# Half-size weight loads in six buffers, and attention bias rows repeated in memory instead of squares made by matmul

## The chip, the core and the metric

The kernel runs on one core of one Trainium2 chip. The metric is the time of one execution on the device in microseconds (us); a lower time is better. Three runs of the kernel before took 2092.91, 2094.27 and 2097.39 us, with a median of 2094.27 us.

## The reference, cut to what matters

Two models run one after the other on 256 tokens of width 1024, all in float32. The first has two layers; each is a mixer (a recurrence, 8 heads of forgetting attention and 4 heads of retention), a cross-attention of 4 heads to a memory of 256 rows, and a gated feed-forward of width 2816. The second has two layers; each is a feed-forward, a mixer (8 heads of sparse attention in three branches, 4 heads of stick-breaking attention, 4 heads of windowed attention) and another feed-forward.

What the change touches in the second model is the table of position biases `rel_bias_2`, 32 buckets by 12 heads. The score of query q and key k of a head gets a bias that depends on the distance q - k alone:

```python
s = (jnp.einsum('bgrqd,bgkd->bgrqk', qb, kb).astype(jnp.float32) * scale
     + head_bias[:, :, t5_bucket(dist)])
```

So the 128 by 256 square of biases of one head is a single row of 383 numbers, each row of the square being that row moved by one place. The same 12 squares serve both layers of the second model.

## The kernel before, in words

**Weights.** Every product with a weight is done as three float32r matmuls: the weight is split into a rounded part `whi` (ACT) and a remainder `wlo` (DVE), the activations into `thi` and `tlo`. The class `Weights` (from line 174) holds the plan. A *chunk* is what one load brings: up to `CHUNK` = 2048 columns per partition, 1 MB, into one of `NRAW` = 3 buffers named `raw`. A *piece* is what one pair of split instructions makes: up to 1024 columns, into one of six `whi`/`wlo` buffers. So most chunks hold two pieces. The loads are issued on SP's queue. `_load` is called for the next chunk when the last piece of a chunk has been split, or, for the four weights of the compression (`nsa_cmp_*_w1_2`, `split=False`, used by the matmuls as they are), when the matmuls have used its last piece. At most six pieces are split ahead of the matmuls. `out_rows` holds the splitting back while it makes a norm.

**Order.** The kernel writes out the order of every engine's instructions itself. The class `Pace` keeps a model of the time on each engine, and `pump` asks it which of the pending *sides* (generators registered with `side`) is due; one of their steps is then put between two matmuls of the main line. Each engine works through its instructions in that order. Pace's model of a load depends on its size, so the order may follow a change in the loads.

**The biases.** In the cross-attention of layer 0 the side `bias_rows` makes the 12 rows and writes them to a memory tensor `ud` (12 by 384). In the cross-attention of layer 1 the side `bias_squares` turns them into 12 squares: for each two heads SP loads 128 rows of 256 numbers from `ud`, each one place after the one before (`hk`), TensorE mirrors them with the matrix `anti`, ACT copies the result (`bts`), and SP stores it in the memory tensor `btiles`. `finish(bias)` makes sure that this is done before `out_rows`. In the mixers of the second model `load_bias` loads one square for a head from `btiles` on ACT's queue into `bt`, 20 times per layer.

**The mixers of the second model.** Their main line is a run of `nat_blocks` and `stat_block` over the columns of `w_in_2`; in the plan (`plan_mixer2`) the four chunks of compression weights stand between chunks of `w_in_2` (`CMP_AT`). The attention heads are sides. All helper instructions carry line 153 in the profile, so instructions are told apart by their tiles.

Of the kernel before, what the change touches and what calls it, by code (L numbers as in the profile page):

```python
# [8 lines left out]
F32 = mybir.dt.float32  # L9
# [11 lines left out]
EPS = 1e-6  # L21
NEG = -1e30
NPIECE = 6
NRAW = 3
PIECE = 1024
CHUNK = 2048

CMP_AT = (1, 3, 5, 7)
RET_HEADS = 4
# [128 lines left out]
class Weights:  # L158
# [10 lines left out]
    def plan(self, ap, c0, c1, k0, k1, a_chunk, a_piece, split=True, gain=None, halves=0, beside=None):  # L169

        b = c1 - c0
        if halves:
            v = ap.rearrange("(g r d) n -> g d r n", g=2, r=halves)
        for k in range(k0, k1, a_chunk):
            a = min(a_chunk, k1 - k)
            ci = len(self.chunks)
            if halves:
                parts = [(slice(64 * g, 64 * g + 64), v[g][:, k : k + a, c0:c1]) for g in (0, 1)]
            else:
                parts = [(slice(0, P), ap[k * P : (k + a) * P, c0:c1].rearrange("(a p) n -> p a n", p=P))]  # L180
            parts = [(ps, slice(0, b), v_) for ps, v_ in parts]
            if beside is not None:
                parts.append((slice(0, P), slice(b, 2 * b), beside[k * P : (k + a) * P, c0:c1].rearrange("(a p) n -> p a n", p=P)))
            self.chunks.append((parts, a, b * (1 if beside is None else 2)))
            for j in range(0, a, a_piece):
                n = min(a_piece, a - j)
                self.pieces.append([ci, j, n, b * (1 if beside is None else 2), split, j + n >= a, None, list(range(k + j, k + j + n)), gain])
# [87 lines left out]
def tile_two_blocks(ctx, tc, I, out):  # L275
    nc = Pace(tc.nc)
# [4 lines left out]
    def nm(s):  # L281
        count[0] += 1
        return f"{s}_{count[0]}"
# [20 lines left out]
    def aux():  # L304
        t = ps_aux.tile([P, 512], F32, tag="aux", name=nm("aux"))
        auxs.append(t.tensor.name)
        return t
# [20 lines left out]
    def mm(ps, a, b, start, stop, beside=False):  # L328

        nc.beside = beside  # L330
        nc.tensor.matmul(ps, a, b, start=start, stop=stop)
        nc.beside = False
# [4 lines left out]
    def side(gen):  # L337
        sides.append([gen, nc.end, False])
# [36 lines left out]
    def finish(gen):  # L375
        while any(i[0] is gen for i in sides):
            pump(force=True)
# [271 lines left out]
    def const(pool, name, dt=F32, tag=None):  # L649
        lo_, hi_ = C128[name]  # L650
        t = pool.tile([P, hi_ - lo_], F32, tag=f"c_{name}", name=nm(name), bufs=1)
        nc.sync.dma_start(t, cst[:, lo_:hi_])
        return t
# [599 lines left out]
    def cross(l, norm, next_maker):  # L1253
        T = norm.T
        with nc.pool(tc, name=nm("cross"), bufs=2) as mp:

            def load_kv(h):
                out_ = []
                for kind in ("k", "v"):
                    t = mp.tile([P, 2, S], F32, tag=f"m{kind}", name=nm(f"m{kind}"))  # L1260
                    nc.scalar.dma_start(t.rearrange("p b n -> p (b n)"), kvd[l, kind][h])
                    out_.append(t)
                return out_

            kv = {h: load_kv(h) for h in (0, 1)}
            heads = {}
            bias = (bias_rows, bias_squares)[l](mp)
            side(bias)
            O = split_T()

            def head(h, qT):
                yield True
                kT, v = kv.pop(h)
                ps = aux()
                for t in (0, 1):
                    for c in (0, 1):
                        mm(ps[:, t * S : (t + 1) * S], qT[:, c, t * P : (t + 1) * P], kT[:, c, :], start=c == 0, stop=c == 1)
                ngm, sums = sm(2, "ngm"), sm(2, "csum")
                nc.vector.tensor_reduce(ngm, ps.rearrange("p (t k) -> p t k", t=2), axis=AX.X, op=ALU.max, negate=True)
                for t in (0, 1):  # L1280
                    nc.vector.tensor_scalar(ngm[:, t : t + 1], ngm[:, t : t + 1], norm.r[t], None, op0=ALU.mult)
                pr = mp.tile([P, 2, S], F32, tag="cpr", name=nm("cpr"))
                for t in (0, 1):
                    nc.scalar.activation(pr[:, t, :], ps[:, t * S : (t + 1) * S], AF.Exp, bias=ngm[:, t : t + 1], scale=norm.r[t], accum_out=sums[:, t : t + 1])
                ri = sm(2, "cri")
                nc.vector.reciprocal(ri, sums)
                for t in (0, 1):
                    nc.vector.tensor_scalar(pr[:, t, :], pr[:, t, :], ri[:, t : t + 1], None, op0=ALU.mult)
                yield True
                ps = aux()  # L1290
                for t in (0, 1):
                    for c in (0, 1):
                        turn(ps[:, c * S + t * P : c * S + (t + 1) * P], pr[:, t, c * P : (c + 1) * P], ident)
                pt = mp.tile([P, 2, S], F32, tag="cpt", name=nm("cpt"))
                nc.scalar.copy(pt.rearrange("p c q -> p (c q)"), ps)
                yield True
                ob = obank(f"o{h % 2}")
                yield from until(nc.free[ob.tensor.name])
                for d in (0, 1):
                    for c in (0, 1):  # L1300
                        mm(ob[:, d * S : (d + 1) * S], v[:, c, d * P : (d + 1) * P], pt[:, c, :], start=c == 0, stop=c == 1)
                ov = ob.rearrange("p (d q) -> p d q", d=2)
                put(O.hi[:, 2 * h : 2 * h + 2, :], O.lo[:, 2 * h : 2 * h + 2, :], ov)
                for kt in (2 * h, 2 * h + 1):
                    O.ready.add((kt, 0))
                    O.ready.add((kt, 1))
                if h < 2:
                    kv[h + 2] = load_kv(h + 2)

            def q_done(h):  # L1310
                def f(a):
                    if h >= 2:
                        finish(heads[h - 2])
                    qT = mp.tile([P, 2, S], F32, tag="cqT", name=nm("cqT"))
                    nc.scalar.activation(qT.rearrange("p c q -> p (c q)"), a[:, :512], AF.Copy, scale=1.0 / 16)
                    heads[h] = head(h, qT)
                    side(heads[h])
                return f

            for h in range(4):  # L1320
                stat_block(T, 2, 2, q_done(h))
            chain = next_maker()
            finish(bias)
            out_rows(lambda k: (O, 0), 8, 4 if units["ffn", l] else 5, chain, units["ffn", l])
        return chain.next

# [25 lines left out]
            nc.scalar.activation(dst.rearrange("p t f -> p (t f)"), a, AF.Sin)  # L1352


    btiles = dpool.tile([12, P, S], F32, tag="btiles", name="btiles")
    bcmp = dpool.tile([P, 240], F32, tag="bcmp", name="bcmp")
    ud = dpool.tile([12, 384], F32, tag="ud", name="ud")
    ucd = dpool.tile([8, 480], F32, tag="ucd", name="ucd")
# [29 lines left out]
                                        cmask[:, t * 15 + n : t * 15 + n + 1].unsqueeze(1).to_broadcast([P, 4, 2]), op=ALU.add)  # L1388
        nc.sync.dma_start(bcmp, bc.rearrange("p t r g n -> p (t r g n)"))

    def bias_squares(bp):

        anti = const(bp, "anti")
        hks = []

        def load(h):
            hk = bp.tile([P, 2, S], F32, tag="hk", name=nm("hk"))
            nc.sync.dma_start(hk, bass.AP(tensor=ud.tensor, offset=ud.offset + h * 384, ap=[[1, P], [384, 2], [1, S]]))
            hks.append(hk)

        load(0)
        for h in range(0, 12, 2):
            if h + 2 < 12:
                load(h + 2)
            yield nc.products + (12.0 if h == 0 else 2.5)
            ps = aux()
            mm(ps, anti, hks.pop(0).rearrange("p h k -> p (h k)"), start=True, stop=True)
            bt = bp.tile([P, 2, S], F32, tag="bts", name=nm("bts"))
            nc.scalar.copy(bt.rearrange("p h k -> p (h k)"), ps)
            nc.sync.dma_start(btiles[h : h + 2].rearrange("h p k -> p h k"), bt)  # L1410

    def plan_mixer2(l):
        w = I["w_in_2"][l]
# [27 lines left out]
    def mixer2(l, T, next_maker):  # L1441
        with nc.pool(tc, name=nm("mix2"), bufs=2) as mp:
# [35 lines left out]

            def load_bias(h):
                t = mp.tile([P, S], F32, tag="bt", name=nm("bt"), bufs=4)  # L1480
                nc.scalar.dma_start(t, btiles[h])
                return t

            def probs(ring, ps, bias, sum_, ngm, first=1e38):
# [491 lines left out]
    for i, (ph, l) in enumerate(phases):  # L1976
        if ph == "mixer1":
            cur = mixer1(l, cur.T, cos, sin, maker(i)).next
        elif ph == "cross":
            cur = cross(l, cur, maker(i))  # L1980
        elif ph == "ffn":
            cur = ffn(cur, maker(i), units["next", l], 960)
        else:
            block1.close()
            if ph == "mixer2":
                cur = mixer2(l, cur.T, maker(i))
            else:
                cur = ffn(cur, maker(i), 0, 128)
# [99 lines left out]
```

## Time and profile before

| what | value |
|---|---|
| median of 3 runs | 2094.27 us (2092.91 to 2097.39) |
| the profiled execution's own time | 2093.85 us |
| its span, first to last instruction | 2092.1 us |
| PE busy | 2038.4 us, 97% of the span |
| DVE, ACT, POOL busy | 1251.7, 1098.7, 89.6 us |
| mean granted TensorE clock | 0.995 |
| DMA moved | 380.79 MB, 182 GB/s; SP's queue 366.46 MB, 52.9% of the 16 DMA engines' span |
| share of the chain that ended last | PE 81%, DVE 6%, ACT 5%, DMA 4%, issue 2% |

PE is TensorE, PEld its weight loads, DVE VectorE, ACT ScalarE, POOL GpSimd, SP the engine that issues loads. The page gives busy time by engine; the chain of waits follows the work that ended last back from the end; a timeline row has the start, the duration, the instruction, and in brackets how long the engine had been idle and what ended that. Matmuls overlap, so one matmul's duration is longer than the step from one to the next. A granted clock of 1.00 stands for 2.4 GHz and 0.50 for 1.2 GHz.

### The profile page before, as it was taken

The numbers are of one execution on the slowest core, as the hardware profiler recorded it, in microseconds if no ns is written. First come the engines' busy times: TensorE is split into PE (matmuls) and PEld (weight loads), VectorE is DVE, ScalarE is ACT, GpSimd is POOL, SyncE is SP. The second block draws the span as 40 slices with busy tenths as digits, with TensorE's granted clock in tenths as the row PEclk, the third lists the DMA queues.
The fourth block names the chain that finished last, engine by engine and source line by source line (L and its number), as shares of the span: only waits on it lengthen the run. The fifth ranks groups of instructions, "written<-read, shape, count | busy, mean of one in ns | idle before, by whom it ended". The sixth has DMA issues, their size and how long they took to land.

```text
span 2092.1 us, 27297 instructions
## 1 busy us (share of the span) xinstructions
PE 2038.4 (97%) x10446; PEld 1675.9 (80%) x10446; DVE 1251.7 (60%) x2123; ACT 1098.7 (53%) x1844; POOL 89.6 (4%) x112
## 2 busy tenths in 40 slices
PE   7999999999999999999999999999999998999999
PEld 6788888888787788788887678888888886778887
DVE  6666565556764755555464667664555565666553
ACT  5556465445564654555445555553554455456542
POOL 0210000001200000000010000000000010000000
PEclk9999999999999999999999999999999999999999
DMA  7555565645465555555555455555555465455552
GB/s 241 184 189 194 184 202 181 219 153 195 162 222 171 184 199 191 165 197 181 204 173 194 137 147 181 192 175 196 181 187 193 163 192 197 132 155 188 176 199 102
DMA packets 200610, 380.79 MB, mean 182 GB/s; under 512 B 14288, under 2 KB 70400, under 8 KB 200480
## 3 DMA queue, kind: packets, MB, share of 16 engines
q1 hardware_dynamic: 188960, 366.46, 52.9%
q10 hardware_dynamic: 11520, 12.59, 1.9%
q8 instruction: 82, 1.34, 0.2%
q14 instruction: 48, 0.39, 0.1%
HBM read 372.03 MB, written 6.99 MB: 181 GB/s over the span
## 4 chain that ended last, share of the span: by engine, by line
PE 81%; DVE 6%; ACT 5%; DMA 4%; issue 2%; POOL 0%; SPq 0%; ACTq 0%; DVEq 0%; POOLq 0%
PE acc L153 73%; PE aux L153 6%; DVE wlo L153 2%; DMA raw<-in_w_in_dram 2%; PE o L153 2%; ACT whi L153 2%; DMA hk<-ud 1%; ACT rn L153 1%; DMA nb<-cdram 0%; ACT thi L153 0%; DVE h L153 0%; DMA bt<-btiles 0%; ACT cpr L153 0%; DMA mem<-in_mem_dram 0%; DVE tlo L153 0%
## 5 line engine op out<-in xcount | busy, mean ns | idle before, releaser
L153 PE MATMUL acc<-whi,thi 128*128 128x512 f32 (+1 forms) x1760 | 702.1, 399 | 4.5 <-ACT kvout L153 2.7
L153 PE MATMUL acc<-wlo,thi 128*128 128x512 f32 (+1 forms) x1760 | 683.0, 388 | 3.5 <-DVE wlo L153 3.3
L153 PE MATMUL acc<-whi,tlo 128*128 128x512 f32 (+1 forms) x1760 | 683.8, 389 | 2.4 <-DVE tlo L153 2.3
L153 DVE TENSOR_TENSOR wlo<-raw,whi 128x1024 fp32r<-128x1024 f32 (+1 forms) x370 | 444.7, 1213 | 313.8 <-ACT whi L153 311.6
L153 ACT CAST whi<-raw 128x1024 fp32r<-128x1024 f32 (+1 forms) x370 | 378.5, 1038 | 252.9 <-PE acc L153 195.5
L153 DVE SCALAR_TENSOR_TENSOR wlo<-raw,prm,whi 128x512 fp32r<-128x512 f32 (+1 forms) x592 | 392.6, 719 | 177.2 <-ACT whi L153 176.9
L153 ACT ACTIVATE whi<-raw,prm 128x512 fp32r<-128x512 f32 (+1 forms) x592 | 372.2, 696 | 92.9 <-PE acc L153 89.4
L153 PEld LDWEIGHTS acc<-whi,thi 128*128 128x128 f32 x1760 | 332.8, 189 | 80.1 <-issue 12.3
L153 PEld LDWEIGHTS acc<-whi,tlo 128*128 128x128 f32 x1760 | 332.2, 189 | 73.2 <-DVE tlo L153 5.5
L153 PEld LDWEIGHTS acc<-wlo,thi 128*128 128x128 f32 x1760 | 333.0, 189 | 67.5 <-DVE wlo L153 6.5
L153 PE MATMUL acc<-whi,ahi 128*128 128x512 f32 x528 | 206.8, 392 | 0.3
L153 PE MATMUL acc<-whi,alo 128*128 128x512 f32 x528 | 205.6, 389 | 0.0
L153 PE MATMUL acc<-wlo,ahi 128*128 128x512 f32 x528 | 205.5, 389 | 0.0
L153 POOL TENSOR_TENSOR r<-v,mhalf 128x1 f32<-128x1 f32 (+3 forms) x46 | 49.5, 1076 | 1661.0 <-DVE v L153 1661.0
L153 DVE SCALAR_TENSOR_TENSOR silu<-acc,r,silu 128x512 f32<-128x512 f32 (+1 forms) x72 | 47.5, 702 | 118.1 <-PE acc L153 94.1
L153 PEld LDWEIGHTS acc<-whi,ahi 128*128 128x128 f32 x528 | 99.1, 188 | 21.6 <-ACT whi L153 1.5
L153 PEld LDWEIGHTS acc<-whi,alo 128*128 128x128 f32 x528 | 99.1, 188 | 20.5
L153 PEld LDWEIGHTS acc<-wlo,ahi 128*128 128x128 f32 x528 | 99.2, 188 | 20.2
L153 PE MATMUL acc<-thi,whi 128*128 128x256 f32 x384 | 113.4, 295 | 0.0
L153 ACT ACTIVATE silu<-acc,r 128x512 f32<-128x512 f32 (+1 forms) x72 | 43.1, 650 | 127.5 <-PE acc L153 127.5
L153 PE MATMUL acc<-tlo,whi 128*128 128x256 f32 x384 | 108.5, 283 | 0.0
L153 PE MATMUL acc<-thi,wlo 128*128 128x256 f32 x384 | 108.5, 282 | 0.0
(299 smaller groups left out, 1823.9 us busy)
## 6 DMA issues: line engine op xcount, KB each, us to landing
raw<-in_w_in_dram SPq DMA_DIRECT2D x65, 1024.0 KB, 5.2
raw<-in_ffn_w_down_dram SPq DMA_DIRECT2D x44, 1024.0 KB, 4.8
raw<-in_ffn_w_gate_dram SPq DMA_DIRECT2D x40, 1024.0 KB, 5.0
raw<-in_ffn_w_up_dram SPq DMA_DIRECT2D x40, 1024.0 KB, 5.0
raw<-in_w_down_dram SPq DMA_DIRECT2D x22, 1024.0 KB, 4.9
raw<-in_w_gate_dram SPq DMA_DIRECT2D x20, 1024.0 KB, 5.0
raw<-in_w_up_dram SPq DMA_DIRECT2D x20, 1024.0 KB, 4.9
raw<-in_w_out_dram SPq DMA_DIRECT2D x16, 1024.0 KB, 4.9
```

The costliest lines, as they stand in the source:

```text
L153: return f(*args, **kwargs)
```

## The change

Two things change. First, a load brings at most 1024 columns, 512 KB, into one of six buffers; `plan` cuts the chunks so that nearly all hold one piece. The memory for `raw` stays the same. Second, `bias_squares` goes, with its matmuls, its copies, `hk`, `bts` and `btiles`. In its place a side `bias_repeats`, started at the feed-forward of layer 0, writes each head's row 128 times into a memory tensor `urep` (12 DMAs on ACT's queue, 10 us apart by Pace's model), and `load_bias` reads its square from `urep` with rows 383 numbers apart, which moves each row by one place.

```diff
-NRAW = 3
+NRAW = 6
-CHUNK = 2048
+CHUNK = 1024
...
     def plan(self, ap, c0, c1, k0, k1, a_chunk, a_piece, split=True, gain=None, halves=0, beside=None):
         b = c1 - c0
+        a_chunk = min(a_chunk, max(1, CHUNK // (b * (1 if beside is None else 2)) // a_piece) * a_piece)
...
-            bias = (bias_rows, bias_squares)[l](mp)
-            side(bias)
+            bias = bias_rows(mp) if l == 0 else None
+            if bias:
+                side(bias)
...
-            finish(bias)
+            if bias:
+                finish(bias)
...
-    btiles = dpool.tile([12, P, S], F32, tag="btiles", name="btiles")
+    urep = dpool.tile([12, P, 384], F32, tag="urep", name="urep")
...
-    def bias_squares(bp):
-        anti = const(bp, "anti")
-        hks = []
-        def load(h):
-            hk = bp.tile([P, 2, S], F32, tag="hk", name=nm("hk"))
-            nc.sync.dma_start(hk, bass.AP(tensor=ud.tensor, offset=ud.offset + h * 384, ap=[[1, P], [384, 2], [1, S]]))
-            hks.append(hk)
-        load(0)
-        for h in range(0, 12, 2):
-            if h + 2 < 12:
-                load(h + 2)
-            yield nc.products + (12.0 if h == 0 else 2.5)
-            ps = aux()
-            mm(ps, anti, hks.pop(0).rearrange("p h k -> p (h k)"), start=True, stop=True)
-            bt = bp.tile([P, 2, S], F32, tag="bts", name=nm("bts"))
-            nc.scalar.copy(bt.rearrange("p h k -> p (h k)"), ps)
-            nc.sync.dma_start(btiles[h : h + 2].rearrange("h p k -> p h k"), bt)
+    def bias_repeats():
+        for h in range(12):
+            nc.scalar.dma_start(urep[h], ud[h, :].partition_broadcast(P))
+            yield nc.products + 10.0
...
-                nc.scalar.dma_start(t, btiles[h])
+                nc.scalar.dma_start(t, bass.AP(tensor=urep.tensor, offset=urep.offset + h * P * 384 + P - 1, ap=[[383, P], [1, S]]))
...
         elif ph == "ffn":
+            if l == 0:
+                side(bias_repeats())
             cur = ffn(cur, maker(i), units["next", l], 960)
```

## Rows read from the trace of the kernel before

**Rows 1.** Waits of PE: who waited for whom: total us, times, longest.

```profile
PE o L153 <- ACT t L153: 7.0, 2, 3.9
PE aux L153 <- DVE nngm L153: 4.8, 2, 2.6
PE aux L153 <- DMA hk<-ud: 2.9, 2, 2.1
PE aux L153 <- ACT cqT L153: 1.8, 3, 1.4
```

**Rows 2.** The chain of waits in the cross-attention of layer 1: start, us.

```profile
630.93 6.42 DMA hk<-ud
```

**Rows 3.** PE's timeline in the same stretch.

```profile
632.08 1.02 PE L153 MATMUL aux<-hk,anti 128*128 128x512 f32 x2
...
633.06 0.28 PE L153 MATMUL acc<-tlo,whi 128*128 128x256 f32 x1
633.18 0.28 PE L153 MATMUL acc<-thi,wlo 128*128 128x256 f32 x1
...
637.39 1.12 PE L153 MATMUL aux<-hk,anti 128*128 128x512 f32 x2 [0.81 <-DMA hk<-ud]
...
648.88 1.10 PE L153 MATMUL aux<-hk,anti 128*128 128x512 f32 x2 [2.09 <-DMA hk<-ud]
```

**Rows 4.** PE's timeline in the two mixers of the second model.

```profile
1127.19 0.48 PE L153 MATMUL aux<-t 64*128 64x256 f32 x1 [2.58 <-DVE nngm L153]
...
1157.01 0.69 PE L153 MATMUL o<-rs,sv 128*64 128x256 f32 x2 [3.87 <-ACT t L153]
...
1735.41 0.50 PE L153 MATMUL aux<-t 64*128 64x256 f32 x1 [2.19 <-DVE nngm L153]
...
1765.88 0.44 PE L153 MATMUL o<-rs,sv 128*64 128x256 f32 x2 [3.10 <-ACT t L153]
```

**Rows 5.** The chain of waits in the first of these mixers: start, us.

```profile
1119.29 4.97 DMA raw<-in_w_in_dram
...
1142.00 5.82 DMA raw<-in_w_in_dram
```

**Rows 6.** ACT's timeline, same mixer.

```profile
1147.84 1.05 ACT L153 CAST whi<-raw 128x1024 fp32r<-128x1024 f32 x1 [5.90 <-DMA raw<-in_w_in_dram]
```

**Rows 7.** SP's timeline, same mixer.

```profile
1119.29 0.37 SPq L153 DMA_DIRECT2D raw<-in_w_in_dram  x1
```

**Rows 8.** Windows: stretch, length, busy of five engines (count), PEclk, DMA share, GB/s.

```profile
1125.00:1135.00 10.00, 7.80 (x53) 6.09 (x54) 5.33 (x16) 6.49 (x18) 0.00 (x0) 0.83 0.53 178
1155.00:1165.00 10.00, 7.99 (x37) 6.50 (x37) 5.02 (x11) 4.39 (x9) 0.00 (x0) 0.66 0.66 209
1735.00:1745.00 10.00, 9.59 (x55) 7.34 (x56) 4.71 (x17) 6.70 (x18) 0.00 (x0) 0.66 0.44 130
1765.00:1775.00 10.00, 9.12 (x53) 7.24 (x54) 5.99 (x12) 5.04 (x10) 0.00 (x0) 0.83 0.60 206
```

**Rows 9.** DMA issues: tile, queue, count, KB each, median us to landing.

```profile
raw<-in_w_in_dram SPq DMA_DIRECT2D x65, 1024.0 KB, 5.2
...
raw<-in_w_gate_dram SPq DMA_DIRECT2D x4, 512.0 KB, 3.9
raw<-in_w_up_dram SPq DMA_DIRECT2D x4, 512.0 KB, 5.1
```

**Rows 10.** PE's timeline at the start of the kernel.

```profile
17.69 0.50 PE L153 MATMUL acc<-wlo,thi 128*128 128x512 f32 x1 [1.13 <-DVE wlo L153]
```

**Rows 11.** The tile `bt`: its loads on ACT's queue (ns min/median/max), and their landing.

```profile
L153 ACTq DMA_DIRECT2D bt<-btiles x40: 326/327/722, 1091.3 to 1840.0; - x40
...
DMA to landing us min/median/max: 2.0/3.8/7.2
```

**Rows 12.** The tile `hk`: landing of its loads, 256 KB each.

```profile
DMA to landing us min/median/max: 4.1/4.7/6.4
```

**Rows 13.** Windows: the gate and up products of layer 0's feed-forward; columns as above.

```profile
275.00:388.00 113.00, 112.86 (x519) 92.95 (x517) 68.43 (x99) 61.46 (x96) 0.00 (x0) 1.00 0.59 195
```

## The prediction

> **What bounds the kernel now.** I read the busy table, then PE's waits, then PE's timeline for every idle gap, then the chain of waits and the other engines' timelines just before the large gaps. PE is busy for 97% of the span, so a change can only win by taking work off PE, by closing one of its few gaps, or by keeping its clock up. The waits name the candidates [rows 1]: PE waits for `t` and `nngm` in the mixers of the second model, and for `hk` in the cross-attention of layer 1.
>
> In that cross-attention the chain runs through a load of `hk` that takes 6.42 us [rows 2]: it is issued on SP behind the store of the pair of squares before. PE's timeline shows PE idle in front of two of the six mirror matmuls, for 0.81 and 2.09 us [rows 3].
>
> In the two mixers PE has one gap of 2.58 and one of 3.87 us, and one of 2.19 and one of 3.10 us [rows 4]. The instructions named there, `nngm` and `t`, stand in the queues of DVE and ACT behind a split that waits for a weight load. In the first mixer the chain goes through loads that take 4.97 and 5.82 us from issue to landing [rows 5], and ACT stands idle for 5.90 us in front of the `whi` at 1147.84 [rows 6]. The reader is to see why: of three buffers, up to two hold compression weights that wait for their matmuls, so the next load starts only when both pieces of the chunk before are split or such a weight is used.
>
> After each of these four gaps the granted clock falls: windows of 10 us around them show 0.83, 0.66, 0.66 and 0.83 [rows 8]. PE has worked at 2.4 GHz up to the gap and then runs for some us at the lower level, 1.2 GHz.
>
> **The change part by part.** The sum is made against the profiled execution's own 2093.85 us, 0.42 below the median of 2094.27; the 1.75 us outside its span stay.
>
> *The squares go.* One pair of mirror matmuls takes PE from 632.08 to the second weight matmul at 633.06, less one step of 0.12 between such matmuls (633.06 to 633.18): 0.86 us [rows 3]. Six of them are 5.2 us, and with the two gaps of 0.81 and 2.09 that is 8.1 us on PE's path. What is late next: the heads. PE already waits for a head's `cqT`, at most for 1.4 us at once [rows 1]; I let one such wait appear and take 6.7 us. Bounds: 3.9 us (such a wait for each of the last three heads) and 8.1. The loads, copies and stores that go with the squares lie on ACT and SP beside PE and count nothing by themselves; the weight loads of this stretch stop queuing behind the stores, but no row shows PE waiting for one there, so I give that nothing.
>
> *Half loads in the mixers.* A half can be issued when one piece is split, one `whi` of 1.05 us [rows 6] or more before the whole chunk could, and 512 KB land in 3.9 us [rows 9]. So the data behind the first kind of gap come 4.97 - 3.9 + 1.05 = 2.1 us sooner, and behind the second kind 5.82 - 3.9 + 1.05 = 3.0 us sooner. Against the gaps of [rows 4] that closes 2.1 + 3.0 in layer 0 and 2.1 + 3.0 in layer 1: 10.2 of 11.7 us. The clock comes on top: the four windows miss (0.17 + 0.34 + 0.34 + 0.17) x 10 = 10.2 us of full clock [rows 8], of which about 1 us falls on idle time (PE is idle for 2.0 us in the second window), so 9.2 us. Without the gaps the reason for the fall is gone, but a faster PE also asks sooner for what ACT and DVE make; of the bounds 0 and 9.2 I take the middle, 4.6. Together 14.8 us; bounds 0 and 20.9.
>
> *Half loads elsewhere.* SP's queue moves 366.46 MB: 349 loads at 1 MB, 699 at 512 KB, so up to 350 more issues of 0.37 us [rows 7], 130 us of SP's time over the whole span. SP does nothing else than issue and wait, and up to six pieces lie between it and PE, so I cost this at nothing; without that cover it would be 0.37 us a load. In a feed-forward DMA has to bring 195 GB/s [rows 13]. Of two loads of 512 KB issued one after the other, the second lands 5.1 + 0.37 - 3.9 = 1.6 us behind the first [rows 7, 9], a rate of 334 GB/s, so the feed-forwards gain and lose nothing. At the start the third piece lands sooner as a half, and PE's gap of 1.13 us [rows 10] can close: 1.1 us, bounds 1.1 gained and 1.1 lost, since later loads now stand ahead of small ones in SP's queue.
>
> A rule speaks against this part. The Trainium skill, "SBUF — State Buffer", section "The DMA setup-cost knee", says that each transfer pays a fixed 2 us or so and that loads should be made as large as they can be. An estimate from that page's fit is 3.2 us for 512 KB and 4.4 us for 1 MB; paid one after another, the 699 halves would take about 2240 us, and the kernel would be slower. The trace has the fixed price in each landing but not in series: the pair just worked out lands 1.6 us apart.
>
> *The rows are repeated.* Twelve issues on ACT's queue during the feed-forward of layer 0. The nearest row is ACT's own issue of `bt`, 0.33 us, at most 0.72 [rows 11]: 4 to 9 us of ACT, which is idle for 113 - 61.5 = 51.5 us of that stretch [rows 13]. They wait for nothing, because `ud` is long written, and ACT's next split is not yet due. The 2.4 MB written and as much read are 40 GB/s over some 120 us beside 195, at a DMA share of 0.59 [rows 13]. Nothing on the path. No row shows a DMA from memory to memory; a hold of ACT is a rival below.
>
> *The squares are read with a slant.* 40 loads of 128 KB, as before, now with rows 1532 bytes apart. Nearest are the overlapping rows of `hk`, 4.7 us for 256 KB [rows 12], against 3.8 for `bt` [rows 11]. I take 0.9 us more at one place in each mixer: 1.8 us lost; bounds 0 and 5.
>
> *The written order.* Pace sees shorter loads and one side less, so steps move. What that costs can't be read from this trace. I bound it by one gap of the largest kind, 3.9 us [rows 4], either way, and take 0.
>
> Sum: 6.7 + 14.8 + 1.1 - 1.8 = 20.8 us, 2093.85 - 20.8 = 2073.05, and 0.42 more for the median: 2073 us.
>
> **The rivals.**
> - *The ring is no deeper.* Four of six half buffers can be held by compression weights just as two of three were, and a load may still be issued too late. Then the mixers gain nothing: 6.7 + 1.1 - 1.8 = 6.0, 2088 us. For it: the memory for `raw` is the same. Against it: a chunk of two pieces frees its first half too late today.
> - *Halves share the lines and only the earlier issue counts.* Each of four gaps shrinks by 1.05 us and the clock still falls: 10.2 us in all, 2084 us. For it: a second 512 KB load takes 5.1 us [rows 9], nearly as long as 1 MB.
> - *The heads were the bound in the cross-attention.* Then the mirror matmuls only filled their waits, and 14.1 us remain, 2080 us. Against it: the gaps wait for `hk` [rows 3].
> - *The new order eats it.* Steps land badly and about 20 us are lost again: 2093 us, no change.
> - *ACT is held (slower).* If a memory-to-memory issue keeps ACT until the data have landed, it costs at the feed-forward of layer 0. It decides from 51.5 / 12 = 4.3 us an issue, where ACT's idle time is used up; at 7.2 us, the slowest landing of `bt` [rows 11], PE loses 12 x 2.9 = 35 us: 2108 us. Against it: an issue of `bt` holds ACT for 0.33 us.
> - *Loads in series (slower), as the page's rule has it.* At 3.9 us each [rows 9], 699 halves take 2726 us. Against it: the pair of [rows 9].
>
> **How the numbers follow.** Forecast 0.47; ring 0.15; halves 0.18; heads 0.07; order 0.07; ACT held 0.04; in series 0.02. The likeliest gives 2073 us. All upper bounds together (8.1 + 20.9 + 1.1 + 3.9 = 34 us) would be 2060; most of that has to come true at once for less than 2063, so the range begins there. It ends at 2089, which takes in the ring rival. Left out are the order rival, both slower ones and the tails. The smallest change that a measurement of this kernel can tell from none is about 0.2%, 4.2 us. Faster by more: 0.47 + 0.15 + 0.18 + 0.07 = 0.87; within: 0.07; slower: 0.06.
>
> **What would show it.** In the profile after, PE's waits should have no row for `hk`, and the stretch of the second cross-attention should be about 7 us shorter. In both mixers the gaps at `nngm` and `t` should be under 1 us, ACT's waits for `raw` well under 5.90 us, and the granted clock 1.00 throughout. In the first feed-forward of layer 0, ACT's queue should show twelve issues of well under 1 us and PE no new wait. I would be wrong if the gaps at `t` stay at 3 us, if PE waits for `bt`, or if a feed-forward becomes longer.

## The result, and the profile after

The changed kernel took 2062.97 us (median of 4 runs, 2062.09 to 2064.04). The kernel before, run on the same chip, took 2095.83 us (4 runs, 2092.91 to 2099.35). The ratio is 0.9848, with a 95% interval of 0.9828 to 0.9867: faster by 32.9 us. The forecast was 2073, a gain of 21 us, with a range from 2063 to 2089; the measured time stands at the low end of it (0.03 us below 2063). So the direction was right, and a term of the sum was too small.

The profiled execution after took 2062.09 us. Four lines of its page, the span, the busy time, SP's queue (packets, MB, share of the DMA engines' span) and the chain by engine:

```profile
span 2060.3 us, 28318 instructions
...
PE 2024.7 (98%) x10434; PEld 1666.6 (81%) x10434; DVE 1250.6 (61%) x2123; ACT 1093.4 (53%) x1838; POOL 88.5 (4%) x112
...
q1 hardware_dynamic: 191136, 363.27, 56.8%
...
PE 88%; DVE 5%; ACT 3%; DMA 2%; issue 2%; SPq 0%; ACTq 0%; DVEq 0%; POOL 0%
```

The span is 2092.1 - 2060.3 = 31.8 us shorter. PE's share of the chain rose from 81 to 88% and that of DMA fell from 4 to 2%, although SP's queue takes more of the DMA engines' time (56.8 for 52.9%).

The waits of PE after (total us, times, longest), against [rows 1]:

```profile
PE aux L153 <- DVE h L153: 11.5, 4, 8.8
PE acc L153 <- DVE wlo L153: 2.5, 5, 0.8
PE aux L153 <- ACT cqT L153: 2.4, 4, 1.4
PE acc L153 <- ACT kvout L153: 2.3, 2, 1.3
```

The rows for `t`, `nngm` and `hk` are gone. What leads is the wait for `h`, nearly all of it for the first input at the start of the kernel; it led before, too (11.6 us). The wait for `cqT` grew by 0.6 us and by one time.

Where the 31.8 us went is read from windows of equal work: a stage runs from the instruction that ends one wait of PE to that which ends another, the same in both kernels. The stages here are the end of the cross-attention of layer 0 with its feed-forward, the mixer and cross-attention of layer 1, and the stretch around the gaps in each mixer of the second model. Columns as in [rows 8]; before:

```profile
225.30:455.72 230.42, 228.96 (x1086) 190.65 (x1086) 134.17 (x200) 121.13 (x192) 4.88 (x9) 1.00 0.55 182
455.72:681.79 226.07, 218.88 (x1312) 185.11 (x1312) 140.26 (x263) 123.83 (x231) 27.10 (x32) 1.00 0.57 189
1062.86:1215.34 152.48, 144.04 (x851) 114.99 (x852) 91.20 (x209) 79.06 (x156) 8.41 (x7) 0.97 0.54 176
1671.46:1824.92 153.46, 144.84 (x851) 115.22 (x851) 91.20 (x209) 79.05 (x156) 8.42 (x7) 0.97 0.54 175
```

and after:

```profile
224.38:454.82 230.44, 228.99 (x1086) 190.64 (x1086) 134.24 (x200) 121.19 (x192) 4.88 (x9) 1.00 0.64 193
454.82:673.73 218.91, 214.75 (x1300) 182.74 (x1300) 140.06 (x263) 120.41 (x225) 27.04 (x32) 1.00 0.58 179
1054.81:1195.60 140.79, 139.36 (x852) 111.52 (x852) 91.11 (x209) 78.67 (x156) 8.43 (x7) 1.00 0.63 193
1651.79:1793.15 141.36, 139.37 (x852) 111.46 (x852) 91.12 (x209) 78.66 (x156) 8.44 (x7) 1.00 0.63 192
```

The first stage did not move (230.42 and 230.44 us), though twelve issues went into ACT's queue there. The second lost 7.16 us. The mixers lost 152.48 - 140.79 = 11.69 and 153.46 - 141.36 = 12.10 us. Together that is 30.95 of 31.8; the start of the kernel gives the other 0.9 (225.30 - 224.38).

The rows of the mixers also split their gain. PE's idle time is the length less the busy time: 8.44 and 8.62 us before, 1.43 and 1.99 after, so 13.6 us came from idle time. The same matmuls were busy for 144.04 and 144.84 us and are now for 139.36 and 139.37: another 10.2 us, and the reason stands in the column of the clock. It was 0.97 over these stretches and is 1.00. The two matmuls that stood behind the gaps of the first mixer now start at 1116.37 and 1140.16 us, without a wait. Windows of 10 us around these places show PE full at 2.4 GHz, where [rows 8] had 0.83 and 0.66:

```profile
1114.00:1124.00 10.00, 10.00 (x83) 8.21 (x82) 5.69 (x19) 7.72 (x19) 0.00 (x0) 1.00 0.90 289
...
1138.00:1148.00 10.00, 10.00 (x68) 7.66 (x65) 6.32 (x13) 5.52 (x10) 0.00 (x0) 1.00 0.59 175
```

ACT's waits for weights of `in_w_in` over the whole kernel (total us, times, longest), before:

```profile
ACT whi L153 <- DMA raw<-in_w_in_dram: 32.5, 16, 5.9
```

and after:

```profile
ACT whi L153 <- DMA raw<-in_w_in_dram: 9.7, 7, 4.1
```

The DMA issues after, columns as in [rows 9]:

```profile
raw<-in_w_in_dram SPq DMA_DIRECT2D x132, 512.0 KB, 4.5
...
bt<-urep ACTq DMA_DIRECT2D x40, 128.0 KB, 3.7
urep<-ud ACTq DMA_DIRECT2D x12, 192.0 KB, 4.3
```

A half load takes 4.5 us for 5.2 of a whole one [rows 9]. The slanted `bt` lands in 3.7 us at the median, where the straight one took 3.8 [rows 11].

### The profile page after: what moved, and what is told of

Same layout as the page of the kernel before. It is cut to its first block, busy times and chain, and to the rows that moved or that the text cites. A ratio compares the mean times of both kernels' runs of the same rounds, so it can differ in the third digit from the quotient of the medians.

```text
span 2060.3 us, 28318 instructions
## 1 busy us (share of the span) xinstructions
PE 2024.7 (98%) x10434; PEld 1666.6 (81%) x10434; DVE 1250.6 (61%) x2123; ACT 1093.4 (53%) x1838; POOL 88.5 (4%) x112
## 3 DMA queue, kind: packets, MB, share of 16 engines
q1 hardware_dynamic: 191136, 363.27, 56.8%
## 4 chain that ended last, share of the span: by engine, by line
PE 88%; DVE 5%; ACT 3%; DMA 2%; issue 2%; SPq 0%; ACTq 0%; DVEq 0%; POOL 0%
PE acc L153 79%; PE aux L153 7%; PE o L153 3%; DVE wlo L153 2%; ACT whi L153 1%; DMA raw<-in_w_in_dram 1%; ACT thi L153 0%; ACT cpr L153 0%; DVE h L153 0%; DVE ngm L153 0%; DMA bt<-urep 0%; DVE rs L153 0%; DVE tlo L153 0%; DVE x L153 0%; DMA mem<-in_mem_dram 0%
```

## The experiments

All ratios are to the kernel before in runs on the same chip; its medians were 2092.47 us (13 runs) beside the first four kernels, 2094.04 (11) beside the next three and 2092.05 (7) beside the last. The first four ran on another chip than the other four, so between kernels of the two groups a difference of medians counts less than the ratios and the windows.

**Each part alone.** The half loads without the change of the biases:

```diff
 # against the kernel before
-NRAW = 3
+NRAW = 6
...
-CHUNK = 2048
+CHUNK = 1024
...
+        a_chunk = min(a_chunk, max(1, CHUNK // (b * (1 if beside is None else 2)) // a_piece) * a_piece)
```

> The kernel before with the half loads in six buffers alone; the squares are still mirrored by matmul. Theory (PE is the path and the parts add): both mixers lose their four gaps and the low clock as in the kernel after, 11.7 and 12.1 us, and the start and first mixer some 1.4 us, so about 25 us below the kernel before, ratio 0.988; the cross-attention of layer 1 keeps its waits for hk and stays about as long as before. Rival (the new source of the bias squares or the side that is gone helped the mixers too): clearly less than 25 us, say 12, ratio 0.994.

Measured: 2070.83 us (2068.06 to 2071.40), ratio 0.9902 (0.9877 to 0.9926). Windows of the same stages, without the first:

```profile
456.65:682.98 226.33, 219.43 (x1312) 185.03 (x1312) 139.97 (x263) 123.77 (x231) 27.01 (x32) 1.00 0.60 187
1064.02:1204.55 140.53, 139.39 (x851) 111.54 (x851) 91.09 (x209) 78.79 (x156) 8.44 (x7) 1.00 0.62 193
1660.72:1802.04 141.32, 139.43 (x851) 111.46 (x852) 91.09 (x209) 78.68 (x156) 8.45 (x7) 1.00 0.61 192
```

The mixers have the whole gain that they have in the changed kernel. The cross-attention's stage has none of it (226.33 for 226.07).

The biases without the half loads:

```diff
 # against the changed kernel
-NRAW = 6
+NRAW = 3
...
-CHUNK = 1024
+CHUNK = 2048
...
-        a_chunk = min(a_chunk, max(1, CHUNK // (b * (1 if beside is None else 2)) // a_piece) * a_piece)
```

> The kernel before with the repeated rows alone; loads of 1 MB in three buffers. Theory: only the cross-attention of layer 1 is shorter, by 6.6 us, ratio 0.997; the four gaps of the mixers stay at 2 to 4 us with the clock falling behind each. Rival (the mirror matmuls only filled waits of the heads): within 2 us of the kernel before, ratio 0.999 to 1.000. The rival that ACT is held would show here as a longer feed-forward of layer 0.

Measured: 2081.77 us (10 runs, 2077.08 to 2087.65), ratio 0.9962 (0.9943 to 0.9980). The two ratios multiply to 0.9864, inside the interval of the whole change, so the parts add up and neither needs the other. The stages of this kernel:

```profile
454.32:673.20 218.88, 214.45 (x1300) 182.90 (x1300) 140.05 (x263) 120.45 (x225) 26.82 (x32) 1.00 0.54 181
1054.24:1204.64 150.40, 143.11 (x852) 114.31 (x852) 91.16 (x209) 79.00 (x156) 8.41 (x7) 0.98 0.55 179
1660.76:1809.69 148.93, 140.48 (x852) 111.67 (x852) 90.98 (x209) 78.83 (x156) 8.42 (x7) 1.00 0.56 180
```

The cross-attention has its full gain (218.88). The mixers keep 7.29 and 8.45 us of idle time, with the gaps of [rows 4] still there in PE's timeline:

```profile
1118.28 1.03 PE L153 MATMUL aux<-t 64*128 64x256 f32 x4 [2.30 <-DVE nngm L153]
...
1147.44 1.12 PE L153 MATMUL o<-rs,sv 128*64 128x256 f32 x4 [3.22 <-ACT t L153]
...
1752.69 0.87 PE L153 MATMUL o<-rs,sv 128*64 128x256 f32 x8 [3.09 <-ACT t L153]
```

The fourth gap, for `nngm` in the second mixer, is 2.48 us. In both mixers PE, ACT and DVE do the same in the same order as in the kernel before. The stretches are still 2.08 and 4.53 us shorter, and 5.3 of these 6.6 us are busy time of the same matmuls: it is the clock, which the profiled execution shows higher here (0.98 and 1.00, for 0.97 twice). The 10 us around the gap of 3.22 us in the first mixer and around the one of 3.09 us in the second:

```profile
1145.00:1155.00 10.00, 7.56 (x41) 5.87 (x43) 5.02 (x11) 5.37 (x9) 0.00 (x0) 0.83 0.63 199
...
1750.00:1760.00 10.00, 7.31 (x52) 5.79 (x53) 5.79 (x13) 6.55 (x12) 0.00 (x0) 1.00 0.60 186
```

PE worked at 2.4 GHz up to both gaps. Behind one the granted clock fell to 0.83 in the mean of the window, behind the other it did not.

**Why half loads help: issued earlier, or landed earlier?** The prediction gave 1.05 us of each gap to a load that is issued earlier, and 1.1 or 1.9 us to one that lands sooner. The next kernel makes the second change alone. A chunk stays 1 MB in one of three buffers, which is freed as a whole, but two DMAs bring its halves.

```diff
 # against the kernel with the biases alone
-        for ps, cs, ap in parts:
-            self.nc.sync.dma_start(v[ps, :, cs], ap)
+        for j in range(0, a, max(1, a // 2)):
+            js = slice(j, min(a, j + max(1, a // 2)))
+            for ps, cs, ap in parts:
+                self.nc.sync.dma_start(v[ps, js, cs], ap[:, js, :])
```

> As e2, but each chunk of 1 MB is brought by two DMAs of 512 KB into the same buffer, issued one behind the other; the buffer still comes free as a whole. Theory (what counts is that a half is issued a piece earlier): the gaps shrink by about 1 us each, and the clock still falls behind the large ones: 2 to 8 us below e2, 2081 to 2087 us. Rival (what counts is that the first half lands sooner): the gaps are gone, 2063 to 2068 us.

Measured: 2069.50 us (2067.81 to 2069.73), ratio 0.9896 (0.9872 to 0.9920). That is 12.3 us below the kernel it was made from. My theory, that the earlier issue is most of it, gave 2081 to 2087 and fell. The rival, with gaps that are gone and 2063 to 2068 us, is much nearer but missed as well, by 1.5 us. The windows of the two mixers:

```profile
1056.42:1199.94 143.52, 140.25 (x851) 111.66 (x852) 90.92 (x209) 78.93 (x156) 8.44 (x7) 1.00 0.58 187
1656.09:1800.84 144.75, 140.38 (x851) 111.65 (x852) 91.01 (x209) 78.93 (x156) 8.45 (x7) 1.00 0.57 186
```

and PE's timeline at the first two gaps:

```profile
1118.83 1.47 PE L153 MATMUL aux<-t 64*128 64x256 f32 x8 [0.62 <-DVE nngm L153]
...
1143.88 0.87 PE L153 MATMUL o<-rs,sv 128*64 128x256 f32 x8 [0.61 <-ACT t L153]
```

The first half is there before the second, the split can begin on it, and the gaps of 2.30 and 3.22 us shrink to 0.62 and 0.61. The chain of waits has the load behind each of these two gaps (start, us), in the kernel with the biases alone

```profile
1110.37 4.98 DMA raw<-in_w_in_dram
...
1133.07 5.17 DMA raw<-in_w_in_dram
```

and here:

```profile
1112.10 3.80 DMA raw<-in_w_in_dram
...
1131.06 3.64 DMA raw<-in_w_in_dram
```

What is waited for lands in 1.18 and 1.53 us less. Counted from the start of the stage, it is also issued 0.45 and 4.19 us earlier, although the buffer is freed as a whole: what came sooner before it was split sooner, and PE had lost less time. So an earlier landing brings an earlier issue with it, and no run has the earlier issue alone. Against the kernel before, whose clock fell behind all four gaps, the mixers are 8.96 and 8.71 us shorter; what is left to the ring freed by halves, with the slightly different order that Pace writes for it, is 2.73 and 3.39. The instructions of PE, ACT and DVE are in the same order here as in the kernel with the biases alone, so none of the 12.3 us comes from the written order.

The Trainium skill, "DMA: Bandwidth & Descriptors", section "Rules for kernel authors", asks for 1 MB and more in a transfer where bandwidth is the aim, and says in another row that the fixed cost overlaps with other work if a transfer is issued early. The first row's aim is not what this kernel lacked: the same bytes as twice as many transfers made it 0.6% faster, since what counts here is when the first piece lands. With the second row these runs agree as far as they go: the cost of the added transfers does not show on PE.

**How many buffers.** The changed kernel with five half buffers, and with four.

```diff
 # against the changed kernel
-NRAW = 6
+NRAW = 5
```

> The kernel after with five half buffers instead of six, less memory than the kernel before had. Theory (the depth of the ring while the compression weights hold up to four buffers decides): one free buffer is left there, gaps of 2 us or more come back in both mixers and the clock falls behind them: 5 to 20 us above the kernel after, 2068 to 2083 us; feed-forwards unchanged. Rival (the finer grain alone decides): within 2 us of the kernel after, 2062 to 2065 us.

Measured: 2068.99 us (2067.46 to 2071.85), ratio 0.9896 (0.9867 to 0.9926), 6 us above the changed kernel. PE and ACT have the same order as in it. The stretches of the two mixers are 143.50 and 144.03 us long, 2.7 us more each, at a clock of 1.00; that is 5.4 of the 7.7 us between the two profiled spans. The wait for `nngm` comes back in both mixers, smaller than expected and with no fall of the clock there:

```profile
1120.08 1.47 PE L153 MATMUL aux<-t 64*128 64x256 f32 x8 [1.28 <-DVE nngm L153]
...
1719.75 1.48 PE L153 MATMUL aux<-t 64*128 64x256 f32 x8 [1.23 <-DVE nngm L153]
```

```diff
 # against the changed kernel
-NRAW = 6
+NRAW = 4
```

> The kernel after with four half buffers. Theory (ring depth while compression weights hold buffers): with 512 KB loads in six, five and four buffers the two mixers lose more each time; with four, all buffers can be held, so gaps of 3 us and more return, the clock falls behind them, and the feed-forwards start to wait as well: 2085 us or more, above five buffers (2069 us) by at least 16 us. Rival (landing time of the half alone matters from five buffers down): within 5 us of five buffers, 2064 to 2074 us.

Measured: 2110.09 us (2102.81 to 2115.24), ratio 1.0073 (1.0050 to 1.0096): slower than the kernel before, which has more memory for `raw`. PE's waits:

```profile
PE aux L153 <- ACT rn L153: 6.3, 2, 3.4
PE aux L153 <- DVE nngm L153: 6.1, 2, 3.2
PE aux L153 <- DVE rn L153: 5.4, 2, 2.7
PE acc L153 <- ACT t L153: 4.9, 2, 2.5
```

With six, five and four half buffers the kernel takes 2063, 2069 and 2110 us. The last step is not clean: Pace wrote a different order for four buffers, on PE and on ACT, so how much of the 41 us is the ring and how much is the order stays open. The step from six to five has one order on PE and ACT.

**The squares: their matmuls or their waits?** The half loads alone, with all loads of `hk` issued at the start of the side:

```diff
 # against the kernel with the half loads alone
-            hk = bp.tile([P, 2, S], F32, tag="hk", name=nm("hk"))
+            hk = bp.tile([P, 2, S], F32, tag="hk", name=nm("hk"), bufs=6)
...
-        load(0)
         for h in range(0, 12, 2):
-            if h + 2 < 12:
-                load(h + 2)
+            load(h)
+        for h in range(0, 12, 2):
             yield nc.products + (12.0 if h == 0 else 2.5)
```

> As e1 (half loads, squares still mirrored), but with a buffer for each pair of squares and all six loads of hk issued at the start, so the matmuls stay and their waits for hk go. Theory (the 6.6 us of the squares are 5.2 us of matmuls and some 2 us of waits): no PE wait for hk, 2 us below e1, about 2069 us. Rival (the wait was no cost of its own, the heads come next): a head's cqT is waited for instead, and the time stays at e1's, 2071 us. A difference of 2 us is at the edge of what the runs can tell; the profile's gaps decide.

Measured: 2067.95 us (2065.99 to 2069.39), ratio 0.9879 (0.9859 to 0.9899). The window of the cross-attention's stage:

```profile
454.27:676.77 222.50, 219.03 (x1311) 184.84 (x1311) 140.06 (x263) 123.71 (x231) 27.35 (x32) 1.00 0.61 190
```

It is 226.33 with the waits for `hk`, 222.50 without them and 218.91 without the squares. So 3.8 us were waits and 3.6 us were the matmuls. Not all of the 3.8 belongs to `hk`, for which PE waited 2.1 us in the kernel with the half loads alone: 0.8 is a wait for `kvout` near 568 us, before the first `hk` is loaded. That wait lies between 0.8 and 2.2 us in the kernels of this study; here it was 1.02 and there 1.78. Without the matmuls PE's busy time is 4.3 us less (219.03 - 214.75), where the prediction had 5.2, and 0.7 us of idle time came back, most of it at `cqT`. Why 4.3 and not 5.2 is open.

**What the clock costs.** The biases alone, with 10 and 13 matmuls of 128x512 that nobody reads put on PE in front of the two waits of each mixer. The gaps are filled and nothing comes earlier.

```diff
 # against the kernel with the biases alone
+            def keep_busy(n, bank):
+                f = bank.pool.tile([P, 512], F32, tag="o0" if bank is ps_o else "aux", name=nm("busy"))
+                for _ in range(n):
+                    nc.nc.tensor.matmul(f, T.hi[:, 0, :P], T.hi[:, 0:2, :].rearrange("p a q -> p (a q)"), start=True, stop=True)
...
                 def scores(b):
+                    if b == 1:
+                        keep_busy(10, ps_o)
...
                         yield from until(hold["sv at"])
+                        keep_busy(13, ps_aux)
```

> As e2 (1 MB loads in three buffers, repeated rows), with 10 and 13 extra matmuls of 128x512, about 2.3 and 3.0 us, written to scratch banks just ahead of the two waits of each mixer, so PE works where it was idle; nothing else moves. Theory (PE's idle time lets the clock fall, and whether it does varies from one execution to the next): granted clock 1.00 in both mixers, time 4 to 6 us below e2's median of 2081.8, so 2076 to 2078 us, and the runs less than 5 us apart where e2's are 10.6 apart. Rival (the clock falls for another reason): falls stay in the mixers, time at e2's or up to 11 us above.

Measured: 2076.58 us (2074.51 to 2078.08), ratio 0.9920 (0.9902 to 0.9939), 5.2 us below the kernel without them, which ran on the other chip; the intervals of the two ratios do not overlap. PE, ACT and DVE have that kernel's order but for the added matmuls. The windows of its mixers:

```profile
1053.72:1201.12 147.40, 145.50 (x874) 115.90 (x875) 90.99 (x209) 78.81 (x156) 8.40 (x7) 1.00 0.56 182
1657.38:1805.55 148.17, 145.63 (x875) 115.94 (x875) 90.98 (x209) 78.81 (x156) 8.41 (x7) 1.00 0.56 181
```

Work that is of no use made the kernel faster, because the clock stays at 2.4 GHz behind it. In these mixers the data come as late as before and the clock does not fall. They are 6.61 and 6.81 us longer than in the changed kernel, which is what lateness costs by itself, and 5.08 and 5.29 us shorter than in the kernel before, which is what the fall cost in its profiled execution. The second mixer of the kernel with the biases alone, where the clock did not fall, agrees: 148.93 us without the added work, 148.17 with it. So 13.4 us are gaps and 10.4 are clock, as the split by PE's busy time has it (13.6 and 10.2).

**Is there more to be had?** The changed kernel with each of its loads of more than one row block brought by two DMAs, so mostly of 256 KB:

```diff
 # against the changed kernel
-        for ps, cs, ap in parts:
-            self.nc.sync.dma_start(v[ps, :, cs], ap)
+        for j in range(0, a, max(1, a // 2)):
+            js = slice(j, min(a, j + max(1, a // 2)))
+            for ps, cs, ap in parts:
+                self.nc.sync.dma_start(v[ps, js, cs], ap[:, js, :])
```

> The kernel after, with each half load of more than one row block brought by two DMAs (256 KB each) into the same buffer. A try at a faster version. Theory (with the mixers' gaps gone PE is the path, and data that land sooner have no gap left to close): within 3 us of the kernel after, 2060 to 2066 us, with ACT's waits for raw in the mixers a little shorter and PE's gaps as they are. Rival (each smaller DMA goes on paying, as from 1 MB to two of 512 KB): 3 us or more below the kernel after. Rival (the price of more DMAs shows): 3 us or more above.

Measured: 2063.07 us (2062.04 to 2063.85), ratio 0.9863 (0.9846 to 0.9879), no faster than 2062.97. ACT's wait for weights in the first mixer fell to

```profile
ACT whi L153 <- DMA raw<-in_w_in_dram: 0.9, 2, 0.7
```

from 2.8 us in the changed kernel, and PE gained nothing: no gap was left there that waits for weights (the stretch of the first mixer is 140.79 us long in both; the second is 142.15 for 141.36, at a clock of 0.99).

## Why the prediction was right in direction and short in size

- **What bounds the kernel.** Right. All of the gain but 0.9 us came from the three stages that the waits of PE named, and the feed-forward of layer 0 did not move. The stretches between the stages shown and behind the last differ by less than 0.1 us.
- **The squares go: 6.7 us predicted, 7.2 measured** in the stage (7.4 between the half loads alone and the whole change). The sum of the ends was 8.1, and one wait of 1.4 us for `cqT` was taken off. That wait came, at 0.6 us. Of the 7.2 us 0.8 is the wait for `kvout` (1.74 us before, 0.96 after), which lies ahead of the squares, so the squares themselves gave some 6.4. The rival by which the heads were the bound would have left nothing here; the run with early `hk` loads shows that 3.6 us of the matmuls were on the path.
- **Half loads in the mixers: 14.8 us predicted, 23.8 measured.** This is the term that was mis-sized, and its upper bound of 20.9 was too low as well. Its two halves were both short. The gaps: 10.2 was 2.1 + 3.0 in each layer, and 13.6 came, since the four gaps of [rows 4], 11.74 us together, closed wholly, and 1.9 us of smaller idle times in the same stretches went with them (waits for `wng`, 1.3 us, and `bc`). The prediction priced each gap by its last load alone; the loads ahead of that one come sooner as well: in the kernel with two DMAs the gap at `t` shrank by 2.61 us, though its own load landed in only 1.53 us less and its buffer was freed as a whole. The clock: the four windows of [rows 8] priced the fall at 9.2 us, and the prediction took half of it, with an argument but no row for the other half; 10.2 came. Had the term stood at its own upper bound, the forecast would have been 2067.
- **By which mechanism.** The prediction gave 4.2 us of the gaps to the earlier issue and 6.0 to the earlier landing. The kernel with two DMAs in a whole chunk shows that landing sooner is where most of it starts: 17.7 us of the 23.8, with the clock that hangs on it and the earlier issue that follows from it. The rival by which halves land no sooner and the clock still falls is refuted. So is the one by which the ring is no deeper and the mixers gain nothing: they gained 23.8 us, and taking one of the six buffers away costs 6.
- **Half loads elsewhere: nothing predicted, nothing found.** More issues on SP lengthened no feed-forward. The rule by which each transfer pays its fixed cost (the Trainium skill, "SBUF — State Buffer", section "The DMA setup-cost knee") was weighed as loads in series, 2726 us by the rows. That page gives its rule for transfers that are bound by DMA; in this feed-forward PE was busy for 112.86 of 113 us at a DMA share of 0.59 [rows 13]. A large part of a landing does not shrink with the bytes (4.5 us for half of them, 5.2 for the whole, both above the estimates of 3.2 and 4.4), but the landings overlap: 699 times 4.5 us would be 3146, more than the whole span.
- **The start: 1.1 us predicted, 0.9 measured.** The stretch up to 224.38 is 0.9 us shorter; PE's wait for `wlo` there is 0.35 us instead of 1.13 [rows 10], so this gap gave 0.8 us and did not close wholly. Other small waits moved both ways (`sc` 1.0 us for 1.9, `kvout` 1.3 for 1.0), so that the sum came so near is in part luck.
- **The rows repeated: nothing predicted, nothing found.** ACT is held for 0.48 us by each of the twelve issues, not 4.3. The tile `urep` after, with its issues on ACT's queue (ns min/median/max, first and last start in us):

```profile
L153 ACTq DMA_DIRECT2D urep<-ud x12: 477/477/562, 263.9 to 374.8; - x12
```

- **The slanted read: 1.8 us lost in the prediction, none found.** `bt` lands as fast as before. The row taken as nearest, `hk` with its 256 KB, has other rows and twice the bytes.
- **The written order: 0 predicted, bounds of 3.9 either way.** No run isolates it for the whole change. In the stretches of the mixers the orders before and after differ little: seven matmuls of each stand in another place, ACT's order is the same. Two of the steps above (the two DMAs in a whole chunk, and the sixth half buffer) moved the time by 12.3 and 6 us without any change of the order on PE and ACT.
- **The chances** went to the right side. The range began at 2063 because less seemed to need all upper ends at once. The mixers alone went past theirs, and that carried the time to the edge. How far also hangs on the clock of the kernel before: in its four runs of 13 at a mean clock of 1.000 it took 2084.16 to 2085.26 us, and against these the change is worth some 21 us. That this is the gain that was forecast is luck, since the forecast had 4.6 us of clock in it.

## What to carry to other kernels

Where a consumer takes a tile in pieces and the bottleneck waits for it, bring the pieces by separate transfers, even into one buffer: the first can be used while the second is on its way. Here that paid from 1 MB to 512 KB, and brought nothing from there to 256 KB, when no such wait was left. Price a gap on TensorE with what the clock loses behind it: where windows around the gaps show the fall, take that price whole unless a row speaks against it, and look at several runs, since the fall does not come in each. Then go through the number of buffers one by one: from five to four the time rose by 41 us, more than the whole change brings, though part of that may be the order.

## What was not expected of the hardware

Whether the clock falls behind a gap of 1 to 4 us is not settled by the gap's length. In one execution the kernel with the biases alone had the fall behind a gap of 3.22 us and not behind one of 3.09 at the same place of the other layer. In the second mixer of the kernel with DMAs of 256 KB the clock fell behind a gap of 1.23 us for `bc` (0.83 in the window from 1775 to 1785 us); the changed kernel has the same gap of 1.23 us at the same place, and its clock stays at 1.00 there. Over the ten runs of the kernel with the biases alone the mean clock went from 0.994 to 1.000 and the time from 2087.65 to 2077.08 us. The runs of the kernel before spread in the same way, from 2084.16 us at a mean clock of 1.000 to 2098.90 at 0.993. The changed kernel, without the four gaps, and the one with matmuls that fill them spread by 2.0 and 3.6 us. So most of what looked like noise of the kernel before was the clock: its median of 2092.47 us beside the first four kernels lies 8 us above its fastest runs there. The Trainium skill, "TensorE: Matmul & The Clock Gate", section "Part 1: The HAM clock gate (the "warmup" mystery)", says that the number of matmuls at the lower clock at a kernel's start differs from run to run; these runs show that in the middle of a kernel, too, the clock can differ from run to run.

A DMA from memory to memory that writes one row of 1.5 KB 128 times held ACT's queue for 0.48 us and landed in 4.3 us, and rows read with a slant of 1532 bytes landed like rows in a line (3.7 and 3.8 us).
